# The mean square of a differential attention head: two transposes and a row sum, or two products with ones

## The chip, the cores and the metric

One core of one Trainium2 chip runs the whole program, one layer of a streaming encoder. The metric is the device time of one execution in microseconds, the median of three runs. In the text PE or TensorE is the matrix engine, DVE or VectorE the vector engine, ACT or ScalarE the activation engine, POOL or GpSimd the general engine, and SP the engine that issues most DMAs.

## The reference

The layer has parallel token mixers, a cross-attention and a gated MLP, over 512 tokens of width 1024 in float32. The change lies in the first mixer, the differential attention with four heads: two softmax maps of a head are subtracted, the difference multiplies the values, and the result of each head and token, 128 numbers, is normalised by its root mean square, with a gain per channel.

```python
def _rms_norm(x, g):
    xf = x.astype(jnp.float32)
    y = xf * lax.rsqrt(jnp.mean(xf * xf, axis=-1, keepdims=True) + EPS)
    return (y * g.astype(jnp.float32)).astype(x.dtype)
...
        p = jax.nn.softmax(jnp.where(mask, s, -jnp.inf), axis=-1)
        a = p[:, :, 0] - lam * p[:, :, 1]
        return jnp.einsum('bhqk,bkhe->bqhe', a.astype(v.dtype), v)
...
        ya = (_rms_norm(ya, diff_norm[l]) * (1.0 - lambda_init)).reshape(B, S, BR_W)
...
        br = jnp.stack([ya, yf, yc, ys], axis=2)
        proj = jnp.einsum('bsnc,ncd->bsnd', br, w_branch[l])
```

The normalised heads are branch a of four; each branch is projected, gated and summed.

## The kernel before

Every float32 matrix product is made of three TensorE products of rounded parts: a high part (rounded to the format that TensorE reads) and a low part (what the rounding left), high by high, high by low, low by high. `split` makes the parts: ScalarE copies to the high one, VectorE subtracts it to get the low one. Weights come in by DMA, are split and used, job after job; `run_blocks` fetches three jobs ahead.

Attention isn't a job of its own. The four heads of branch a are background tasks (`a_task`), put in a queue when their q and k columns are ready; between jobs `bg.tick()` lets at most two tasks take steps, by a clock of the TensorE work issued. The order of instructions on each engine is settled when the program is built, by a scheduler over the whole program; on the chip each engine takes its own list in that order and waits where an operand isn't ready.

A task has six steps. In steps 0 to 3 it makes scores of 128 queries against 128 to 512 keys (two maps, banks `sc`), reads them with mask and maximum (L831), takes exponentials (L836), scales (L840) and subtracts (L841). In steps 1 to 4 the difference is transposed (bank `tr`, L236) and split into `pth` and `ptl`. In steps 3 and 5 these multiply the values into one bank `av`, so that `av` at the end holds the head's output turned: 128 channels on the partitions, 512 tokens along the free dimension. The mean square is over the channels, and so over the partitions.

The kernel before turns it: the copy at L846 takes `av` to SBUF, four transposes bring the tokens to the partitions, ScalarE squares (L852), VectorE sums along the free dimension (L854), GpSimd adds EPS and raises to the power -0.5 (`rstd_of`, L268 and L271, 128 x 4), VectorE multiplies (L856), four transposes turn it back, and a split with the gain `half["dn"]` (L158 and L159) writes the branch's parts `y["a"]`, tiles `y8b`.

Buffers matter here. `e4()` gives one of three SBUF buffers of 128 x 2 x 512, which scores, differences and outputs of all heads share. There are two banks each of `mm`, `av`, `tr` and `sc`. While the heads run, gate and branch products use `mm` alone; when the heads are through, the products for the values of the second attention (`vf_jobs`) use `mm` and `av`, and then its tasks (`f_task`) begin, whose bias tiles GpSimd makes from rows `crows`, which it stores and loads by DMA (L943, L960, L990, L992). Branch a's projections (`gate_blocks(0, "a")`) come after the first q and k columns of that attention. GpSimd also clears parts of the `qk` tiles (L760).

Of the kernel before, what the change touches and what calls it, by code (L numbers as in the profile page):

```python
# [17 lines left out]
F32 = mybir.dt.float32  # L18
F32R = mybir.dt.float32r
AF = mybir.ActivationFunctionType  # L20
ALU = mybir.AluOpType
AX = mybir.AxisListType
# [3 lines left out]
P = 128  # L26
S = 512
D = 1024
NT = S // P
# [54 lines left out]
def hybrid_layer(ctx: ExitStack, tc: tile.TileContext, a: dict, out: bass.AP):  # L84
    nc = tc.nc
    V, A, G, PE, SP = nc.vector, nc.scalar, nc.gpsimd, nc.tensor, nc.sync
# [10 lines left out]
    def bank(tag=None):  # L97
        if tag is None:
            turn_of.n += 1
            tag = "av" if turn_of.shared and turn_of.n % 2 else "mm"  # L100
        return psum.tile([P, 512], F32, tag=tag, name=f"ps_{tag}", bufs=2)
# [13 lines left out]
    nhalf = gp.tile([P, 8], F32, name="nhalf")  # L115
    G.memset(nhalf[:, :4], -0.5)
    G.memset(nhalf[:, 4:], EPS)
    eps = nhalf[:, 4:]
# [33 lines left out]
    def split(ps, hi, lo, scale=None):  # L152

        if scale is None:
            A.copy(hi, ps)  # L155
            V.tensor_tensor(lo, ps, hi.bitcast(F32), ALU.subtract)  # L156
        else:
            A.activation(hi, ps, AF.Copy if isinstance(scale, float) else AF.Identity, scale=scale)  # L158
            V.scalar_tensor_tensor(lo, ps, scale, hi.bitcast(F32), ALU.mult, ALU.subtract)  # L159
# [71 lines left out]
    def matmul(ps, lhs, rhs, start, stop):  # L231
        PE.matmul(ps, lhs, rhs, start=start, stop=stop)  # L232
        bg.clock += max(int(math.prod(rhs.shape[1:])), 256) * 0.00042

    def transpose(ps, x, n=P):
        PE.transpose(ps, x, ident[:n, :n])  # L236
        bg.clock += 0.107
# [26 lines left out]
    def rstd_of(pool, parts, n=1):  # L264

        m = pool.tile([P, n], F32, tag="st_m", name="st_m", bufs=4)
        r = pool.tile([P, n], F32, tag="st_r", name="st_r", bufs=4)
        G.tensor_tensor(m, parts[0], eps[:, :n], ALU.add)  # L268
        for part in parts[1:]:
            G.tensor_tensor(m, m, part, ALU.add)  # L270
        G.tensor_tensor(r, m, nhalf[:, :n], ALU.pow)  # L271
        return r
# [33 lines left out]
    m1p = m1.__enter__()  # L306
# [6 lines left out]
    def e4(dtype=F32):  # L313
        return m1p.tile([P, 2, S], dtype, tag="e", name="e", bufs=3)
# [191 lines left out]
    half = {}  # L506
# [77 lines left out]
    def y8b():  # L584
        return m2bp.tile([P, 4, S], F32R, tag="y8b", name="y8b", bufs=2)

    acc = [m2p.tile([P, S], F32, tag=f"acc{m}", name=f"acc{m}") for m in range(NK)]
    y = {}
# [191 lines left out]
    def scores(ps, qk, c, q0, w):  # L780

        q = slice(q0, q0 + P)
        matmul(ps[:, :w], qk[:, c, q], qk[:, 2 + c, :w], True, False)
        matmul(ps[:, :w], qk[:, c, q], qk[:, 4 + c, :w], False, True)

    def to_keys_major(e, n, pt_h, pt_l, local):

        ps = bank("tr")
        for kt in range(n):
            transpose(ps[:, kt * P:(kt + 1) * P], e[:, kt * P:(kt + 1) * P])  # L790
        sl = slice(local * P, (local + 1) * P)
        split(ps[:, :n * P].rearrange("p (k c) -> p k c", k=n), pt_h[:, :n, sl], pt_l[:, :n, sl])

    def values(ps, terms, pt, half):


        n = 2 * half + 2
        for kt in range(n):
            q0 = P if kt == n - 1 else 0
            passes = terms(kt)  # L800
            for i, (v, p) in enumerate(passes):
                matmul(ps[:, half * 256 + q0:half * 256 + 256], v, pt[p][:, kt, q0:256],
                       kt == 0 and i == 0, kt == n - 1 and i == len(passes) - 1)

    def pt_tiles():
        return (m1p.tile([P, 4, 256], F32R, tag="pth", name="pth", bufs=2),
                m1p.tile([P, 4, 256], F32R, tag="ptl", name="ptl", bufs=2))


    def a_task(h, qk, v):  # L810
        es, pt, av = {}, None, None
        for step in range(6):
            if step in (3, 5):
                if av is None:
                    av = bank("av")
                vh, vl = (x[:, :, h * P:(h + 1) * P] for x in v[0])
                values(av, lambda kt: ((vh[:, kt], 0), (vh[:, kt], 1), (vl[:, kt], 0)), pt, step // 2 - 1)
            cost = 0.0
            if 1 <= step <= 4:
                if step in (1, 3):  # L820
                    pt = pt_tiles()
                to_keys_major(es.pop(step - 1)[:, 0], step, pt[0], pt[1], (step - 1) % 2)
                cost += 0.1 + 0.15 * step
            if step < 4:
                qt, w = step, (step + 1) * P
                e = es[qt] = e4()
                st = m1p.tile([P, 8], F32, tag="st8", name="st8", bufs=4)
                for c in range(2):
                    ps = bank("sc")
                    scores(ps, qk, c, qt * P, w)  # L830
                    V.tensor_tensor_reduce(e[:, c, :w], ps[:, :w], mask_a[:, S - w:], scale=1.0,  # L831
                                           scalar=-3.0e38, op0=ALU.add, op1=ALU.max,
                                           accum_out=st[:, c:c + 1])
                V.tensor_scalar(st[:, 2:4], st[:, 0:2], -HD ** -0.5, None, ALU.mult)
                for c in range(2):
                    A.activation(e[:, c, :w], e[:, c, :w], AF.Exp, bias=st[:, 2 + c:3 + c],  # L836
                                 scale=HD ** -0.5, accum_out=st[:, 4 + c:5 + c])
                V.reciprocal(st[:, 6:8], st[:, 4:6])
                V.tensor_scalar(st[:, 7:8], st[:, 7:8], lam, None, ALU.mult)
                A.activation(e[:, 1, :w], e[:, 1, :w], AF.Copy, scale=st[:, 7:8])  # L840
                V.scalar_tensor_tensor(e[:, 0, :w], e[:, 0, :w], st[:, 6:7], e[:, 1, :w], ALU.mult,  # L841
                                       ALU.subtract)
                cost += 0.6 + 0.0035 * w
            if step == 5:
                e = e4()
                A.copy(e[:, 0], av)  # L846
            yield cost, 3.5

        ps = bank("tr")
        for t in range(NT):  # L850
            transpose(ps[:, t * P:(t + 1) * P], e[:, 0, t * P:(t + 1) * P])
        A.activation(e[:, 1], ps, AF.Square, scale=1.0 / math.sqrt(P))  # L852
        ms = m1p.tile([P, NT], F32, tag="ms4", name="ms4", bufs=2)
        V.tensor_reduce(ms, e[:, 1].rearrange("p (t c) -> p t c", t=NT), AX.X, ALU.add)  # L854
        r = rstd_of(m1p, [ms], NT)
        V.tensor_tensor(e[:, 0].rearrange("p (t c) -> p t c", t=NT),  # L856
                        ps.rearrange("p (t c) -> p t c", t=NT),
                        r.unsqueeze(2).to_broadcast([P, NT, P]), ALU.mult)
        yield 1.5, 3.5
        ps2 = bank("tr")  # L860
        for t in range(NT):
            transpose(ps2[:, t * P:(t + 1) * P], e[:, 0, t * P:(t + 1) * P])
        if "a" not in y:
            y["a"] = (y8b(), y8b())
        split(ps2, y["a"][0][:, h], y["a"][1][:, h], half["dn"])
        yield 0.6, 0.0


    crows = dram.tile([8, S], F32, name="crows")
# [192 lines left out]
    def mixer_jobs():  # L1062
# [23 lines left out]
        for h, n in enumerate((0, 2, 4, 6)):  # L1086
            yield from qk_jobs(O_AQ, O_AK, h, lambda qk, h=h: bg.add(a_task(h, qk, va), "a"))
            if n:
                yield then(lambda: bg.drain("conv"))
            for _ in range(n):  # L1090
                yield next(gc)
# [651 lines left out]
```

## Time and profile before

| | |
|---|---|
| Time, median of three runs | 1065.24 us (1065.16 to 1066.46) |
| Profiled execution: span | 1064.1 us, 1.1 us less than that median |
| TensorE busy | 1052.2 us, 99% of the span |
| VectorE, ScalarE, GpSimd busy | 796.6, 497.5, 147.8 us |
| HBM traffic | 142 GB/s over the span |

The profile is of one execution. Busy time is that of an engine's own instructions; in the slices a digit is the busy share in tenths of one fortieth of the span, 26.6 us. In a timeline row the bracket gives the idle time of the engine ahead of the row and what ended it. A group's row gives the busy time of all its instructions, the mean of one in ns, and the idle time ahead of them. The profile lists no time of this execution other than its span; what lies around the span is taken from the median.

### The profile page before, as it was taken

The numbers are of one execution on the slowest core, as the hardware profiler recorded it, in microseconds if no ns is written. First come the engines' busy times: TensorE is split into PE (matmuls) and PEld (weight loads), VectorE is DVE, ScalarE is ACT, GpSimd is POOL, SyncE is SP. The second block draws the span as 40 slices with busy tenths as digits, with TensorE's granted clock in tenths as the row PEclk, the third lists the DMA queues.
The fourth block names the chain that finished last, engine by engine and source line by source line (L and its number), as shares of the span: only waits on it lengthen the run. The fifth ranks groups of instructions, "written<-read, shape, count | busy, mean of one in ns | idle before, by whom it ended". The sixth has DMA issues, their size and how long they took to land.

```text
span 1064.1 us, 14583 instructions
## 1 busy us (share of the span) xinstructions
PE 1052.2 (99%) x5375; PEld 895.3 (84%) x5375; DVE 796.6 (75%) x1262; ACT 497.5 (47%) x819; POOL 147.8 (14%) x249
## 2 busy tenths in 40 slices
PE   9999999999999999999999999999999999999997
PEld 8888888888888978888888899999888888888886
DVE  6999997567666357776675888786778787777796
ACT  5322222367465255645443565664333333445662
POOL 4000000000001015332110031021111211111001
PEclk9999999999999999999999999999999999999999
DMA  8954333322222242332344754225576766725672
GB/s 264 300 155 103 104 96 99 97 82 80 80 80 63 58 139 79 100 99 80 119 125 140 268 159 120 80 75 190 180 228 218 237 219 216 235 82 179 204 219 81
DMA packets 162108, 152.58 MB, mean 143 GB/s; under 512 B 5567, under 2 KB 135212, under 8 KB 162037
## 3 DMA queue, kind: packets, MB, share of 16 engines
q1 hardware_dynamic: 152995, 119.91, 37.4%
q10 hardware_dynamic: 6482, 23.21, 5.8%
q0 software_dynamic: 2560, 8.54, 2.8%
q8 instruction: 42, 0.69, 0.3%
q14 instruction: 29, 0.24, 0.1%
HBM read 133.79 MB, written 17.84 MB: 142 GB/s over the span
## 4 chain that ended last, share of the span: by engine, by line
PE 93%; issue 3%; DMA 1%; ACT 1%; DVE 1%; POOL 0%; POOLq 0%; DVEq 0%; SPq 0%; ACTq 0%
PE ps_mm L232 50%; PE ps_av L232 29%; PE ps_sc L232 7%; PE ps_tr L232 4%; PE ps_tr L236 3%; DMA wide<-in_w_out 1%; DMA ck<-crows 0%; PE ps_mm L384 0%; DMA crows<-e 0%; PE ps_sc L389 0%; DVE nt L281 0%; POOL st_r L271 0%; ACT hth L432 0%; ACT wa L412 0%; ACT wh L190 0%
## 5 line engine op out<-in xcount | busy, mean ns | idle before, releaser
L190 ACT CAST wh<-wr 128x1024 fp32r<-128x1024 f32 (+1 forms) x142 | 148.7, 1050 | 273.1 <-PE ps_mm L232 181.1
L191 DVE TENSOR_TENSOR wl<-wr,wh 128x1024 fp32r<-128x1024 f32 (+1 forms) x142 | 178.2, 1256 | 89.4 <-ACT wh L190 89.1
L232 PE MATMUL ps_mm<-hth,wh 128*128 128x512 f32 (+1 forms) x616 | 231.4, 382 | 0.6 <-DVE qk L765 0.3
L232 PE MATMUL ps_mm<-htl,wh 128*128 128x512 f32 (+1 forms) x616 | 230.2, 380 | 0.0
L232 PE MATMUL ps_mm<-hth,wl 128*128 128x512 f32 (+1 forms) x616 | 229.9, 380 | 0.0
L232 PEld LDWEIGHTS ps_mm<-hth,wh 128*128 128x128 f32 x616 | 114.1, 188 | 21.7 <-ACT hth L155 0.8
L232 PEld LDWEIGHTS ps_mm<-hth,wl 128*128 128x128 f32 x616 | 114.0, 188 | 21.1
L232 PEld LDWEIGHTS ps_mm<-htl,wh 128*128 128x128 f32 x616 | 114.2, 188 | 20.4
L232 PE MATMUL ps_av<-hth,wh 128*128 128x512 f32 (+1 forms) x328 | 122.6, 374 | 0.0
L232 PE MATMUL ps_av<-htl,wh 128*128 128x512 f32 (+1 forms) x328 | 122.5, 374 | 0.0
L232 PE MATMUL ps_av<-hth,wl 128*128 128x512 f32 (+1 forms) x328 | 122.5, 373 | 0.0
L664 DVE SCALAR_TENSOR_TENSOR y<-y,par,y 128x482 f32<-128x482 f32 (+29 forms) x120 | 83.9, 743 | 0.2
L232 PEld LDWEIGHTS ps_av<-hth,wl 128*128 128x128 f32 x328 | 61.6, 188 | 10.9
L232 PEld LDWEIGHTS ps_av<-htl,wh 128*128 128x128 f32 x328 | 61.6, 188 | 10.9
L232 PEld LDWEIGHTS ps_av<-hth,wh 128*128 128x128 f32 x328 | 61.7, 188 | 10.7
L1536 DVE TENSOR_TENSOR wl<-dw,wh 128x1024 fp32r<-128x1024 f32 x32 | 40.2, 1261 | 12.2 <-ACT wh L1535 12.0
L1535 ACT CAST wh<-dw 128x1024 fp32r<-128x1024 f32 x32 | 33.4, 1051 | 22.6 <-PE ps_tr L232 7.5
L990 POOL TENSOR_SCALAR fbias<-ck,cq 128x128 f32<-128x128 f32 (+3 forms) x32 | 27.5, 865 | 69.0 <-DVE st L996 61.8
L1484 ACT ACTIVATE th<-c 128x512 f32<-128x512 f32 x22 | 13.9, 631 | 48.5 <-DVE c L594 45.6
L155 ACT CAST pth<-ps_tr 128x512 fp32r<-128x512 f32 (+3 forms) x56 | 23.4, 448 | 22.0 <-PE ps_tr L236 21.8
L594 DVE SCALAR_TENSOR_TENSOR c<-ps_mm,par,c 128x510 f32<-128x510 f32 (+1 forms) x44 | 32.7, 744 | 0.7
L156 DVE TENSOR_TENSOR ptl<-ps_tr,pth 128x512 fp32r<-128x512 f32 (+3 forms) x56 | 27.9, 512 | 6.0 <-ACT pth L155 5.7
(471 smaller groups left out, 2105.2 us busy)
## 6 DMA issues: line engine op xcount, KB each, us to landing
wr<-in_w_up SPq DMA_DIRECT2D x44, 512.0 KB
wr<-in_w_in SPq DMA_DIRECT2D x38, 512.0 KB
wr<-in_w_gate SPq DMA_DIRECT2D x32, 512.0 KB
wp<-in_w_down ACTq DMA_DIRECT2D x22, 512.0 KB
sums<-wp ACTq DMA_DIRECT2D x22, 512.0 KB
dw<-sums SPq DMA_DIRECT2D x44, 256.0 KB
wr<-in_w_branch SPq DMA_DIRECT2D x16, 512.0 KB
wide<-in_w_out SPq DMA_DIRECT2D x12, 512.0 KB
```

Source lines behind the costliest of these rows:

```text
L155: A.copy(hi, ps)
L156: V.tensor_tensor(lo, ps, hi.bitcast(F32), ALU.subtract)
L190: order(A.copy(hi, raw[:, :n]))
L191: low.tensor_tensor(lo, raw[:, :n], hi.bitcast(F32), ALU.subtract)
L232: PE.matmul(ps, lhs, rhs, start=start, stop=stop)
L236: PE.transpose(ps, x, ident[:n, :n])
L594: ins = V.scalar_tensor_tensor(dst[:, s:], src[:, :S - s], w(k), dst[:, s:], ALU.mult, ALU.add)
L664: ins = V.scalar_tensor_tensor(dst[:, s:], src[:, :S - s], pc("conv_dw", k * 4 + j), dst[:, s:], ALU.mult, ALU.add)
L990: G.tensor_scalar(bias[:, :w], ck[j][:, :w], -1.0, cq[:, qt, head:head + 1], ALU.mult, ALU.add)
L1484: A.activation(th, c[:, 0], AF.Tanh, scale=0.5)
L1535: A.copy(hi, x)
L1536: V.tensor_tensor(lo, x, hi.bitcast(F32), ALU.subtract)
```

## The change

In step 5 the head's output isn't copied. ScalarE squares `av` with the factor 1/128 into `e`, rounds it to the high part in a second buffer `sq`, and VectorE makes the low part. Two products with a 128 x 128 tile of ones (written by GpSimd into the place in `y["a"]` that the head's result will take later) sum both parts over the partitions, in a bank `sc`; every partition then holds the mean square of all 512 tokens. ScalarE adds EPS on the way to SBUF, GpSimd raises the 128 x 512 tile to -0.5, and VectorE multiplies `av` by the gain and this tile, and the result is split. The eight transposes, the row sum and `rstd_of` are gone; `av` is read a second time at the end.

```diff
             if step == 5:
-                e = e4()
-                A.copy(e[:, 0], av)
+                e, sq = e4(), e4(F32R)
+                if "a" not in y:
+                    y["a"] = (y8b(), y8b())
+                G.memset(y["a"][0][:, h, :P].bitcast(F32), 1.0)
+                A.activation(e[:, 0], av, AF.Square, scale=1.0 / math.sqrt(P))
+                A.copy(sq[:, 0], e[:, 0])
+                V.tensor_tensor(sq[:, 1], e[:, 0], sq[:, 0].bitcast(F32), ALU.subtract)
             yield cost, 3.5
 
-        ps = bank("tr")
-        for t in range(NT):
-            transpose(ps[:, t * P:(t + 1) * P], e[:, 0, t * P:(t + 1) * P])
-        A.activation(e[:, 1], ps, AF.Square, scale=1.0 / math.sqrt(P))
-        ms = m1p.tile([P, NT], F32, tag="ms4", name="ms4", bufs=2)
-        V.tensor_reduce(ms, e[:, 1].rearrange("p (t c) -> p t c", t=NT), AX.X, ALU.add)
-        r = rstd_of(m1p, [ms], NT)
-        V.tensor_tensor(e[:, 0].rearrange("p (t c) -> p t c", t=NT),
-                        ps.rearrange("p (t c) -> p t c", t=NT),
-                        r.unsqueeze(2).to_broadcast([P, NT, P]), ALU.mult)
-        yield 1.5, 3.5
-        ps2 = bank("tr")
-        for t in range(NT):
-            transpose(ps2[:, t * P:(t + 1) * P], e[:, 0, t * P:(t + 1) * P])
-        if "a" not in y:
-            y["a"] = (y8b(), y8b())
-        split(ps2, y["a"][0][:, h], y["a"][1][:, h], half["dn"])
-        yield 0.6, 0.0
+        ps = bank("sc")
+        for i in range(2):
+            matmul(ps, y["a"][0][:, h, :P], sq[:, i], i == 0, i == 1)
+        A.activation(e[:, 0], ps, AF.Identity, bias=eps[:, :1])
+        G.tensor_tensor(e[:, 0], e[:, 0], nhalf[:, :1].to_broadcast([P, S]), ALU.pow)
+        yield 0.8, 3.5
+        V.scalar_tensor_tensor(e[:, 1], av, half["dn"], e[:, 0], ALU.mult, ALU.mult)
+        split(e[:, 1], y["a"][0][:, h], y["a"][1][:, h])
+        yield 2.0, 0.0
```

## The prediction

> **What bounds the kernel now.** I read the page first: busy times, the slices, then the chain that ended last.
>
> ```profile
> span 1064.1 us, 14583 instructions
> PE 1052.2 (99%) x5375; PEld 895.3 (84%) x5375; DVE 796.6 (75%) x1262; ACT 497.5 (47%) x819; POOL 147.8 (14%) x249
> POOL 4000000000001015332110031021111211111001
> PEclk9999999999999999999999999999999999999999
> PE 93%; issue 3%; DMA 1%; ACT 1%; DVE 1%; POOL 0%; POOLq 0%; DVEq 0%; SPq 0%; ACTq 0%
> ```
>
> TensorE is busy for 99% of the span and carries 93% of the chain; GpSimd is nearly idle. Whatever keeps TensorE fed costs nothing, and whatever takes its next instruction away costs its full length. 0.2% (about 2 us) is what a measurement of this kernel can tell from no change.
>
> Next the timeline of GpSimd around the four differential heads, where the change works. Columns: start, length, engine, line, instruction, and in brackets the idle time before it.
>
> ```profile
> 265.45 1.09 POOL L760 MEMSET qk<- 64x512 f32 x2 [14.87 <-issue]
> 274.02 1.46 POOL L271 TENSOR_TENSOR st_r<-st_m,nhalf 128x4 f32<-128x4 f32 x1
> 292.98 1.01 POOL L271 TENSOR_TENSOR st_r<-st_m,nhalf 128x4 f32<-128x4 f32 x1
> 329.77 1.01 POOL L271 TENSOR_TENSOR st_r<-st_m,nhalf 128x4 f32<-128x4 f32 x1
> 356.81 1.01 POOL L271 TENSOR_TENSOR st_r<-st_m,nhalf 128x4 f32<-128x4 f32 x1
> 388.39 0.57 POOL L943 DMA_DIRECT2D crows<-e  x1 [30.58 <-DVE e L942]
> ```
>
> The four powers to -0.5 (one a head, four columns each) lie 274 to 358 us, with GpSimd idle between them. The change makes each 512 columns wide. So the whole forecast hangs on what a power costs per column.
>
> **The price of the power.** The groups by form (busy us, mean ns) and two single rows:
>
> ```profile
> L271 POOL TENSOR_TENSOR st_r<-st_m,nhalf 128x1 f32<-128x1 f32 x30 | 19.7, 659 | 1.6
> L271 POOL TENSOR_TENSOR st_r<-st_m,nhalf 128x4 f32<-128x4 f32 x4 | 4.5, 1122 | 0.3
> L268 POOL TENSOR_TENSOR st_m<-ms,nhalf 128x4 f32<-128x4 f32 x4 | 0.8, 202 | 66.9 <-DVE ms L854 49.6 <-DVE st L834 17.2
> L415 POOL TENSOR_TENSOR wa<-e,wa 128x512 fp32r<-128x512 f32 x4 | 5.1, 1297 | 1.4 <-ACT wa L412 1.4
> 16.65 0.55 POOL L271 TENSOR_TENSOR st_r<-st_m,nhalf 128x1 f32<-128x1 f32 x1
> 17.16 0.19 POOL L268 TENSOR_TENSOR st_m<-st_s,nhalf 128x1 f32<-128x1 f32 x1
> ```
>
> An addition costs 0.19 us for one column and 0.20 for four: width is free there. The power costs 0.55 us for one and 1.01 for four (three of four; the fourth, 1.46, lifts the mean): 0.153 us for each further column, and the means give the same slope, (1122 - 659) / 3 = 154 ns. Carried to 512 columns: 0.55 + 511 x 0.153 = 78.7 us. No row shows a wide power, so I bound it: below by a two-operand 512-column subtraction, 1.30 us; above by all of 1.01 us scaled by 128, 129 us. I take 78.7, the row nearest in operation; the subtraction is another operation, whose own slope is not that of the power.
>
> The Trainium skill, page "GPSIMD Engine Reference", section "3.1 Elementwise — side-by-side cycle accounting", counts about 2.6 cycles an element at 1.2 GHz for a two-operand elementwise operation; by it, as an estimate, the power would take about 1.1 us and the kernel would come out as in rival A. The subtraction's row fits that rule; the power's rows don't.
>
> **Part 1, TensorE's own work.** Out go eight transposes a head, in come two 512-column products. The chain of before in order of time (start, length, count) has their pitch:
>
> ```profile
> 254.93 3.40 PE ps_mm L232 x15
> 258.33 0.71 PE ps_sc L232 x4
> 270.04 0.77 PE ps_tr L236 x7
> 320.51 1.23 PE ps_av L232 x11
> ```
>
> A 512-column product is 0.227 us, a 384-column one 0.18, a transpose 0.11, a product of 128 to 264 columns 0.11. So 0.88 - 0.45 = 0.43 us less a head, 1.7 us in all. This is the only gain.
>
> **Part 2, the small steps.** Gone from ScalarE and VectorE are the copy, square, reduction, multiplication and the scaled split; new are the square, the two-part rounding of it, the addition of EPS, one multiplication and a split. The nearest rows:
>
> ```profile
> L846 ACT COPY e<-ps_av x4: 575/587/589, 266.8 to 351.6; 128x512 f32<-128x512 f32 x4
> L158 ACT ACTIVATE y8b<-ps_tr,s_dn x4: 672/688/690, 281.6 to 361.6; 128x512 fp32r<-128x512 f32 x4
> L155 ACT CAST y8b<-e x4: 612/620/621, 82.0 to 130.2; 128x512 fp32r<-128x512 f32 x4
> L156 DVE TENSOR_TENSOR y8b<-e,y8b x4: 705/713/722, 84.9 to 132.3; 128x512 fp32r<-128x512 f32 x4
> L841 DVE SCALAR_TENSOR_TENSOR e<-e,st 128x512 f32<-128x512 f32 x4 | 3.0, 749 | 0.3 <-ACT e L840 0.3
> ```
>
> ScalarE goes from three passes of 0.6 to 0.7 us to four, VectorE keeps three of about 0.7: under 1 us a head, beside engines at 47% and 75%. Counted at nothing, since TensorE's products cover it. The memsets of ones (0.2 us each) stand far ahead on GpSimd, also at nothing.
>
> **Part 3, what waits for the power.** In the order in which the changed kernel is built, GpSimd runs the four powers as one chain, and three things hang on each: the head's `av` bank, which now stays in use until the last multiplication (before, the copy at L846 freed it); its `e` buffer, one of three; and VectorE's queue, where that multiplication waits with the next head's score reads behind it. Head 2's first score read stands behind head 0's multiplication, and its reading frees the `sc` bank for head 1's sum. So the power of head 1 can't begin before that of head 0 has ended, and so for heads 1 and 2. Between two powers lie multiplication 0.75, split 0.62 + 0.71, two score reads with their two exponentials (their groups stand under rival A, with means of 0.49 and 0.56 us over all widths; for 128 and 256 columns I take 1.7 and 2.2 in all), and the EPS addition 0.69: 4.5 and 5.0 us. Head 3's input is ready in time; only three memsets (1.6 us) lie before its power. Behind the last come 0.75 + 0.62 = 1.4 us until the first product of branch a. Length of the chain: 4 x 78.7 + 4.5 + 5.0 + 1.6 + 1.4 = 327 us.
>
> What TensorE can do meanwhile is read off that order, with the pitches above:
> - behind head 0's power, up to head 1's sum: 252 products of 512 columns and 68 narrow ones, 57.2 + 7.6 = 64.8 us
> - behind the powers of heads 1 and 2, up to the first `av` product of the f values, which needs head 2's bank: 14 wide, 8 of 384, 116 narrow, 3.2 + 1.4 + 13.0 = 17.6 us. The remaining attention of heads 2 and 3 stands here with few other products between
> - behind head 3's power, up to the first branch-a product: 144 wide, 108 narrow, 32.7 + 12.1 = 44.8 us
>
> 327 - 127 = 200 us are left in which TensorE has nothing to do. GpSimd's DMAs of `crows` and the f bias are queued behind the last power too, but come before TensorE needs more.
>
> **Part 4, TensorE's clock.** The same six products at the start and a few microseconds later:
>
> ```profile
> 1.33 2.93 PE L384 MATMUL ps_mm<-e,ones 128*128 128x256 f32 x6 [1.33 <-DVE e L335]
> 6.69 1.46 PE L384 MATMUL ps_mm<-e,ones 128*128 128x256 f32 x6
> ```
>
> From rest they take twice as long. Four long rests follow here, each with about 1.5 us of such a restart, up to 3 if a slow stretch is longer; some of it falls where ScalarE and VectorE are late anyway. I take 4 us, between 0 and 12. The Trainium skill, page "TensorE: Matmul & The Clock Gate", section "What's actually happening", has the array at half its clock after an idle window of about 3.4 us and for about 3.4 us of work; by that the four restarts would be at most 7 us. The rows agree in the factor, though the slices' granted clock, quoted above, shows full speed there.
>
> **Sum.** The profiled span of 1064.1 us lies 1.1 us under the median of 1065.24; I keep that distance. 1065.2 - 1.7 + 200 + 4 = 1267.5, so 1268 us.
>
> **Rivals.** For a power of p us the same count gives: behind head 0, p + 1 - 65 where positive; behind heads 1 and 2, 2p + 10 - 18, but at least about 22 (rival A); behind head 3, p + 3 - 45, but at least about 5.
>
> A, the power costs as an addition does. For it: an addition's width is free. Against: the two power rows. It would still be slower, because the attention of heads 2 and 3 now stands packed:
>
> ```profile
> L831 DVE CUSTOM_DVE_ANT_0 e<-ps_sc,mask_a 128x128 f32<-128x128 f32 (+3 forms) x32 | 14.7, 488 | 4.7 <-PE ps_sc L232 4.7
> L836 ACT ACTIVATE e<-e,st 128x128 f32<-128x128 f32 (+3 forms) x32 | 17.7, 556 | 6.8 <-DVE st L834 6.8
> L840 ACT ACTIVATE e<-e,st 128x128 f32<-128x128 f32 (+3 forms) x16 | 9.0, 562 | 5.3 <-DVE st L839 5.2
> L841 DVE SCALAR_TENSOR_TENSOR e<-e,st 128x128 f32<-128x128 f32 (+3 forms) x16 | 8.7, 548 | 2.2 <-ACT e L840 2.1
> ```
>
> These four groups alone are 50.1 us for four heads, 25 for two, one after the other in each step; with the small steps and the transposed splits it is about 40 us against 17.6 of products: some 22 lost, and 5 more behind head 3. 1065 - 2 + 27 = 1090 us, between 1075 and 1100.
>
> B, a wide power runs at half the price a column, about 40 us (its loop may fill better than four columns show). 0 + 72 + 5: 1065 - 2 + 77 = 1140 us. Nothing in the trace speaks for it but that no width above four is shown.
>
> C, the work above one addition grows by groups of four, (1.01 - 0.20) / 4 = 0.20 us a column, 104 us. 40 + 200 + 62: 1065 - 2 + 302 + 4 = 1369 us. Against: the first column would then be as dear as four, and it is not.
>
> D, the other side: the power is cheap and TensorE finds its queue full throughout, so that only part 1 counts: 1065.2 - 1.7 = 1063.5 us. It decides so only if a power stays under about 10 us and the packed attention runs with gate products between. The idle GpSimd speaks for it; the built order, with 17.6 us of products beside two heads of attention, against.
>
> **How the numbers follow.** Forecast 0.75, with its own range 1250 to 1290 (a power of 75 to 83 us, a restart of 0 to 12). A 0.06, B 0.10, C 0.06, D 0.03. For 8 in 10 I reach into B's upper half (a power of 53 us gives 0 + 98 + 11, about 1176 with the restart) and a little above the linear price (86 us, about 1300): 1175 to 1300. Faster is D alone; the chance of no difference is a remainder between D and A: 0.02, 0.01, 0.97.
>
> **What would show it.** In the profile after: four GpSimd rows of 128x512 near 79 us each, nearly end to end from about 277 us (the 274 of before and a longer chain ahead of it) to about 604, GpSimd's busy time up by about 312 us; four long waits of TensorE, near 15, twice 60 to 70 with short ones between, and near 30 us, each released by the steps behind a power; TensorE's products otherwise at 0.227 us; all as before after the first branch-a product. A power of a few microseconds, or TensorE waiting on something else in that stretch, would make it wrong.

## The result, and the profile after

The changed kernel takes 1275.87 us (median of four runs, 1274.94 to 1276.07) where the kernel before takes 1065.23 (1065.16 to 1066.46) beside it. The ratio is 1.198, 95% interval 1.196 to 1.200: slower by 210.6 us. The profiled executions have spans of 1273.2 and 1064.1 us, 209.1 us apart.

The page of the changed kernel: busy times, the slices of TensorE, of GpSimd and of the granted clock (one fortieth of the span is 31.8 us here), and the shares of the chain that ended last.

```profile
PE 1072.9 (84%) x5351; PEld 906.7 (71%) x5351; DVE 800.7 (63%) x1262; ACT 501.4 (39%) x823; POOL 469.1 (37%) x249
PE   9999999999740060295599999999999999999997
POOL 3000010039989989999733200030211211111001
PEclk9999999999955565598799999999999999999999
PE 71%; POOL 19%; issue 8%; DVE 1%; ACT 0%; POOLq 0%; DVEq 0%; ACTq 0%
```

In a stretch of some 340 us GpSimd's digits stand at 7 to 9. TensorE's fall there to 0 in three slices and to between 2 and 7 in six others, and stay at 9 in two. GpSimd, which had 0% of the chain, holds 19%. Outside that stretch the rows look like before's.

GpSimd's timeline in that stretch (start, length, engine, line, instruction; in brackets the idle time before it; left out are three short memsets, ahead of the third and of the fourth power):

```profile
277.19 81.95 POOL L858 TENSOR_TENSOR e<-e,nhalf 128x512 f32<-128x512 f32 x1 [11.09 <-issue]
363.71 81.92 POOL L858 TENSOR_TENSOR e<-e,nhalf 128x512 f32<-128x512 f32 x1 [4.58 <-ACT e L857]
...
450.73 81.92 POOL L858 TENSOR_TENSOR e<-e,nhalf 128x512 f32<-128x512 f32 x1 [3.94 <-issue]
...
534.23 81.91 POOL L858 TENSOR_TENSOR e<-e,nhalf 128x512 f32<-128x512 f32 x1
```

Four powers of 81.9 us, nearly end to end from 277.19 to 616.14 us, on an engine whose four powers took 4.5 us before. What TensorE does meanwhile is in the rows that follow its long waits (the number in brackets is the wait), and in the windows by stage (length, then the busy time of PE, PEld, DVE, ACT and POOL, granted clock, DMA share, GB/s):

```profile
361.68 1.22 PE L232 MATMUL ps_sc<-e,y8b 128*128 128x512 f32 x2 [20.55 <-DVE st L831]
448.41 1.19 PE L232 MATMUL ps_sc<-e,y8b 128*128 128x512 f32 x2 [67.30 <-DVE st L831]
533.48 0.59 PE L232 MATMUL ps_av<-wh,hth 128*128 128x264 f32 x1 [59.21 <-DVE e L860]
617.62 1.65 PE L232 MATMUL ps_mm<-y8b,wh 128*128 128x512 f32 x3 [27.31 <-ACT y8b L155]
```

```profile
277.00:361.00 84.00, 64.13 (x315) 54.11 (x313) 28.27 (x32) 21.35 (x28) 81.95 (x1) 0.90 0.25 75
361.00:446.00 85.00, 14.75 (x51) 10.79 (x51) 12.50 (x48) 11.44 (x33) 82.23 (x2) 0.52 0.00 0
446.00:533.00 87.00, 19.37 (x87) 15.86 (x87) 12.11 (x35) 11.23 (x27) 82.94 (x4) 0.56 0.00 0
533.00:618.00 85.00, 53.85 (x271) 46.06 (x272) 26.06 (x42) 24.68 (x35) 83.62 (x5) 0.82 0.22 62
```

The four waits make 174.4 us. None of them names GpSimd: TensorE waits for VectorE and ScalarE. The engine behind them is found one step further back, in what the last multiplication (L860) waited for:

```profile
  POOL e L858: 168.9, 4
```

In the two middle stages TensorE works 14.75 of 85 and 19.37 of 87 us, at a granted clock of 0.52 and 0.56; VectorE and ScalarE are idle too, and almost nothing moves on the DMA queues. Everything stands behind GpSimd.

### The profile page after: what moved, and what is told of

Read it like the earlier page. It is cut to its first block, busy times and chain, and to the rows that moved or that the text cites. A ratio compares the mean times of both kernels' runs of the same rounds, so it can differ in the third digit from the quotient of the medians.

```text
span 1273.2 us, 14547 instructions
## 1 busy us (share of the span) xinstructions
PE 1072.9 (84%) x5351; PEld 906.7 (71%) x5351; DVE 800.7 (63%) x1262; ACT 501.4 (39%) x823; POOL 469.1 (37%) x249
## 4 chain that ended last, share of the span: by engine, by line
PE 71%; POOL 19%; issue 8%; DVE 1%; ACT 0%; POOLq 0%; DVEq 0%; ACTq 0%
PE ps_mm L232 35%; PE ps_av L232 23%; POOL e L858 19%; PE ps_sc L232 6%; PE ps_tr L232 3%; PE ps_tr L236 2%; PE ps_mm L442 0%; PE ps_av L442 0%; PE ps_mm L384 0%; PE ps_sc L389 0%; DVE wl L191 0%; DVE e L860 0%; ACT y8b L155 0%; DVE o L1629 0%; ACT wh L190 0%
## 5 line engine op out<-in xcount | busy, mean ns | idle before, releaser
L858 POOL TENSOR_TENSOR e<-e,nhalf 128x512 f32<-128x512 f32 x4 | 327.7, 81924 | 19.6 <-issue 15.0
L860 DVE SCALAR_TENSOR_TENSOR e<-ps_av,s_dn,e 128x512 f32<-128x512 f32 x4 | 3.0, 751 | 168.9 <-POOL e L858 168.9
L232 PE MATMUL ps_av<-wh,hth 128*128 128x512 f32 (+2 forms) x74 | 26.0, 363 | 62.5 <-DVE e L860 59.2
L232 PE MATMUL ps_sc<-e,y8b 128*128 128x512 f32 x8 | 4.0, 572 | 87.9 <-DVE st L831 87.9
L155 ACT CAST y8b<-e 128x512 fp32r<-128x512 f32 x8 | 4.9, 618 | 177.6 <-DVE e L860 175.7
L232 PEld LDWEIGHTS ps_av<-wh,hth 128*128 128x128 f32 x74 | 15.0, 203 | 64.7 <-DVE e L860 59.4
```

The costliest lines, as they stand in the source:

```text
L858: G.tensor_tensor(e[:, 0], e[:, 0], nhalf[:, :1].to_broadcast([P, S]), ALU.pow)
L860: V.scalar_tensor_tensor(e[:, 1], av, half["dn"], e[:, 0], ALU.mult, ALU.mult)
```

## The experiments

All start from the changed kernel, except the last. Each kernel's order of instructions is built anew, so the work that lies beside a power differs from one to the next.

**The root on ScalarE.** The rest of the change stays.

```diff
-        A.activation(e[:, 0], ps, AF.Identity, bias=eps[:, :1])
-        G.tensor_tensor(e[:, 0], e[:, 0], nhalf[:, :1].to_broadcast([P, S]), ALU.pow)
+        A.activation(e[:, 0], ps, AF.Ln, bias=eps[:, :1])
+        A.activation(e[:, 0], e[:, 0], AF.Exp, scale=-0.5)
```

> The root is taken on ScalarE (logarithm of the mean square plus EPS, then the exponential of -0.5 times it, two passes over 128 x 512) and GpSimd does none of it; the rest is as in the changed kernel. Theory (the power on GpSimd, 81.92 us each, is the whole loss): two passes of about 0.7 us in place of 81.92, TensorE never rests long, so 1065.2 less the 1.7 us of the transposes, with small losses: 1062 to 1068 us, and the four long TensorE waits are gone. Rival A (what costs is that the heads stand packed and that each hands on to the next): about 1090 us, with the waits behind the score reads still there. Rival of the functions (changing between logarithm and exponential costs ScalarE time): gaps or long rows at those two passes; at over 5 us a head it would show as 1075 us or more.

Measured: 1062.96 us against 1065.82 for the kernel before on the same chip, ratio 0.9974 (0.9966 to 0.9983): faster than both kernels, by 2.9 us against before (1.8 to 3.6 by the interval). What differs is the medians: single runs of the kernel before went there from 1061.51 to 1067.12 us, and of this one from 1061.89 to 1063.86. The whole loss hangs on the one instruction. The span is 1062.1 us; the busy times of its page, and then the two groups of table loads on ScalarE (busy us, mean ns of one):

```profile
PE 1051.0 (99%) x5351; PEld 893.6 (84%) x5351; DVE 798.5 (75%) x1262; ACT 513.0 (48%) x835; POOL 143.6 (14%) x245
```

```profile
L857 ACT ACT_TABLE_LOAD x4 | 5.1, 1283 | 1.0 <-PE ps_sc L232 1.0
L858 ACT ACT_TABLE_LOAD x4 | 5.1, 1283 | 0.1
```

TensorE is back at 99%. The rival of the functions holds in part: each change between logarithm and exponential loads a table, 1283 ns, eight times. That is 10.3 us of ScalarE and costs nothing, because ScalarE, busy 48% of the span, isn't what TensorE waits for.

The Trainium skill, page "ScalarE: Activation LUTs", section "Table sets: the hidden batching unit", has logarithm and exponential in one set, so that one load would do for both; in this run each change had its load.

**A multiplication in place of the power.**

```diff
-        G.tensor_tensor(e[:, 0], e[:, 0], nhalf[:, :1].to_broadcast([P, S]), ALU.pow)
+        G.tensor_tensor(e[:, 0], e[:, 0], nhalf[:, :1].to_broadcast([P, S]), ALU.mult)
```

> The 128 x 512 operation on GpSimd is a multiplication by the same operand instead of a power, so the root is left out; place, width, engine and operands are the same. Theory (the price of the power per column): the four operations take 1.3 us each, as the 512-column subtraction on that engine did, instead of 81.92, and the time is 1063 to 1068 us. Rival (any 512-column operation of GpSimd in this place is slow, or the handing over between heads costs): over 1090 us.

Measured: 1063.92 us, ratio 0.9991 (0.9977 to 1.0004). The group of the multiplications (busy us, mean ns of one, then idle time before):

```profile
L858 POOL TENSOR_TENSOR e<-e,nhalf 128x512 f32<-128x512 f32 x4 | 4.2, 1041 | 62.2 <-ACT e L857 51.1 <-issue 11.1
```

1.04 us where the power takes 81.92, on the same engine, with the same operands, in the same place of the program; the kernel leaves the root out. So neither GpSimd as such nor the row of steps around it is dear, but this operation. The estimate of 1.1 us that the prediction worked out from the Trainium skill, page "GPSIMD Engine Reference", section "3.1 Elementwise — side-by-side cycle accounting", is near the 1.04 us of the multiplication and short by a factor of 74 for the power.

**Half the columns.**

```diff
-        G.tensor_tensor(e[:, 0], e[:, 0], nhalf[:, :1].to_broadcast([P, S]), ALU.pow)
+        G.tensor_tensor(e[:, 0, :256], e[:, 0, :256], nhalf[:, :1].to_broadcast([P, 256]), ALU.pow)
```

> The power is taken over 256 of the 512 columns; the other tokens keep the mean square without a root. Theory (0.160 us a column, one chain): four rows of 41 us; by the prediction's count 0 behind head 0, 2 x 41 + 10 - 18 = 74 behind heads 1 and 2, 5 behind head 3, so 1065 - 2 + 79 = 1142 us, from 1127 if the packed stretch loses less. Rival (loss in proportion to the power): half of 210 us, 1170 us. Rival (a fixed price for an instruction, width free): 1276 us.

Measured: 1126.49 us, ratio 1.0572 (1.0553 to 1.0591), at the lower end of what was expected (1142, from 1127) and far from both rivals. Halving the powers takes away 149 of 211 us, not half: cover comes off first. The group of the powers, and the windows of this kernel (columns as above):

```profile
L858 POOL TENSOR_TENSOR e<-e,nhalf 128x256 f32<-128x256 f32 x4 | 164.5, 41124 | 26.8 <-issue 15.0 <-ACT e L857 11.8
```

```profile
270.00:318.00 48.00, 48.00 (x223) 39.95 (x222) 23.14 (x33) 19.09 (x28) 40.95 (x1) 1.00 0.29 84
...
330.00:371.00 41.00, 21.15 (x122) 18.31 (x120) 14.49 (x42) 12.45 (x30) 41.00 (x1) 0.74 0.10 26
...
376.00:417.00 41.00, 16.98 (x83) 14.18 (x83) 8.95 (x25) 8.95 (x22) 40.80 (x1) 0.62 0.00 1
417.00:460.00 43.00, 38.31 (x208) 33.21 (x209) 19.75 (x35) 16.86 (x25) 42.89 (x6) 0.95 0.30 86
```

The price is linear: 41.12 and 81.92 us, 0.159 us for each column between them. Head 0's power is hidden whole, as the count had it (TensorE busy 48 of 48 us), and head 3's costs 4.7 us where the count said 5. In the middle the count, 74 us, was too high: TensorE stands idle 19.9 and 24.0 us beside the two powers and some 3 between them, 47 in all. What it does there runs at 0.74 and 0.62 of the clock, and that makes its busy time 13 us longer over the span (1063.5 against 1050.3 us with the multiplication). 47 + 5 + 13 = 65 us, near the 62.6 by which the span exceeds that with the multiplication (1061.7). The 17.6 us of cover were counted for the order with 512 columns; in this one more work lies beside the second power (122 instructions, where the changed kernel has 51).

**The bank freed early.**

```diff
                 V.tensor_tensor(sq[:, 1], e[:, 0], sq[:, 0].bitcast(F32), ALU.subtract)
+                A.copy(e[:, 1], av)
...
-        V.scalar_tensor_tensor(e[:, 1], av, half["dn"], e[:, 0], ALU.mult, ALU.mult)
+        V.scalar_tensor_tensor(e[:, 1], e[:, 1], half["dn"], e[:, 0], ALU.mult, ALU.mult)
```

> ScalarE copies av to SBUF behind the square, and the last multiplication reads the copy, so that the av bank is free before the power. Theory (the chain of the four powers ends last, and what is freed inside it only lets TensorE run ahead to the next wait): the time stays at 1276 us within 5, the 59 us wait of the av product goes, and another wait, at the first product of branch a, grows by about as much. Rival (the held av bank costs by itself): 59 us less, about 1217 us.

Measured: 1276.3 us, ratio to before 1.1975 (1.1954 to 1.1997): no change. TensorE's waits (in all, times, longest), and the windows of the last two powers:

```profile
PE ps_mm L232 <- ACT y8b L155: 93.4, 2, 79.2
PE ps_sc L232 <- DVE st L831: 87.9, 2, 67.3
```

```profile
446.00:533.00 87.00, 66.01 (x347) 56.40 (x347) 32.99 (x71) 34.82 (x61) 82.95 (x4) 0.87 0.21 61
533.00:618.00 85.00, 3.91 (x11) 2.26 (x11) 4.68 (x6) 1.24 (x2) 83.89 (x5) 0.50 0.00 0
```

The 59 us wait of the `av` product is gone, TensorE works 66 us beside the third power instead of 19, and then has 4 us left beside the fourth instead of 54. The sum of the waits is 181 us where it was 174. The wait that was taken away named a bank; its length was set by GpSimd, and it came back at the next door.

**One power alone**, for head 0 (shown) and, in a second kernel, for head 3; the other heads take the root on ScalarE.

```diff
-        A.activation(e[:, 0], ps, AF.Identity, bias=eps[:, :1])
-        G.tensor_tensor(e[:, 0], e[:, 0], nhalf[:, :1].to_broadcast([P, S]), ALU.pow)
+        A.activation(e[:, 0], ps, AF.Identity if h == 0 else AF.Ln, bias=eps[:, :1])
+        if h == 0:
+            G.tensor_tensor(e[:, 0], e[:, 0], nhalf[:, :1].to_broadcast([P, S]), ALU.pow)
+        else:
+            A.activation(e[:, 0], e[:, 0], AF.Exp, scale=-0.5)
```

> The power on GpSimd for head 0 alone (81.92 us); heads 1 to 3 take the root on ScalarE by logarithm and exponential. Theory (a power costs its length less the TensorE work that the order leaves beside it): by the prediction's count 82 + 1 - 65 = 18 us behind head 0 alone, so 1063 + 18 = 1081 us, and up to 1107 where the three heads behind it then stand packed. Rival (each power costs the same, a quarter of the 210 us): 1063 + 53 = 1116 us. Rival (one power is hidden, only the chain of four costs): 1063 us.

> The power on GpSimd for head 3 alone; heads 0 to 2 take the root on ScalarE. Theory (length less cover): 82 + 3 - 45 = 40 us behind head 3, all of it in one wait of TensorE at the first product of branch a: 1063 + 40 = 1103 us, and none behind the other heads. Rival (each power costs the same): 1116 us. Rival (only the chain of four costs): 1063 us.

Measured: head 0 alone 1108.5 us, ratio 1.0418 (1.0397 to 1.044); head 3 alone 1104.95 us, ratio 1.038 (1.036 to 1.04). The second meets its forecast of 1103; the first lies just above the upper end of its range, 1107. Head 3's kernel: the power takes 81.95 us from 362.80 us on; the window of the work beside it, and TensorE's longest wait:

```profile
363.00:413.00 50.00, 48.70 (x257) 41.22 (x255) 23.14 (x38) 23.82 (x34) 50.00 (x1) 1.00 0.34 98
```

```profile
PE ps_mm L232 <- ACT y8b L155: 33.1, 1, 33.1
```

Some 50 us of work lie beside the power, where 45 were counted in the order of the changed kernel, then TensorE waits 33.1 us for the end. The span, 1103.1 us, is 41.0 above that with no power (1062.1), and the count said 40. Of the 8 us that are not in this wait, 4.9 are TensorE's busy time (1055.9 against 1051.0 us), longer at the lower clock behind it; the other 3 no single wait names. Head 0's kernel:

```profile
277.00:360.00 83.00, 64.31 (x316) 54.27 (x314) 27.77 (x31) 20.92 (x27) 81.95 (x1) 0.92 0.26 76
360.00:420.00 60.00, 46.17 (x239) 38.66 (x240) 29.46 (x97) 37.11 (x78) 2.59 (x5) 0.69 0.03 8
```

```profile
PE ps_sc L232 <- DVE st L831: 24.8, 5, 20.6
```

A wait of 20.6 us where the count said 18, and then a second loss. In the 60 us after the power TensorE is idle for 13.8 us, 12 of them behind that wait, and works at a clock of 0.69, which makes its busy time 14 us longer over the span (1065.1 against 1051.0 us). The span is 44.8 us above that with no power, so 24 lie beyond the wait: 14 of busy time and 10 more of idle time over the whole span. That fits the mechanism of the prediction's rival A, the attention of the heads packed behind one another with too few products between, which it priced at 22 us for two heads; here three heads stand behind the power. No run separates it from other reasons. The two kernels lose nearly the same, 44.8 and 41.0 us, but not in the same way: a wait of 20.6 us and 24 behind it, or a wait of 33.1 and 8. So the two times alone would not refute an equal price for each power; that the cost isn't in proportion is shown by the kernels with 256 and with 64 columns. The two kernels together lose 86 of the 211 us; if the losses add, 125 are left to the two powers in the middle, which have little work beside them. A power has no price of its own for the kernel: it costs its length less the cover at its place, and what it crowds together behind it.

**Sixty-four columns.**

```diff
-        G.tensor_tensor(e[:, 0], e[:, 0], nhalf[:, :1].to_broadcast([P, S]), ALU.pow)
+        G.tensor_tensor(e[:, 0, :64], e[:, 0, :64], nhalf[:, :1].to_broadcast([P, 64]), ALU.pow)
```

> The power over 64 of the 512 columns (the other tokens keep the mean square without a root). Theory (0.160 us a column, cover of 18 to 65 us a power): four rows of 10.2 us, all nearly covered: 1064 to 1070 us. This is also the point from which the rival D of the prediction was to hold (a power under about 10 us). Rival (packed heads cost by themselves): 1090 us.

Measured: 1067.73 us, ratio 1.0025 (1.0012 to 1.0039).

```profile
L858 POOL TENSOR_TENSOR e<-e,nhalf 128x64 f32<-128x64 f32 x4 | 42.1, 10528 | 54.6 <-ACT e L857 43.5 <-issue 11.1
```

At 10.5 us a power the kernel is 2.6 us slower than before, and some 5 slower than with the root on ScalarE. With 1.04 us an operation (the multiplication) the interval still holds no difference. So a power begins to cost before its length reaches the 18 to 65 us of products that were counted beside it. No wait of TensorE in this kernel is longer than 1.4 us, but the stretch with the heads shows where it falls back:

```profile
250.00:420.00 170.00, 165.13 (x880) 141.02 (x879) 100.71 (x228) 90.98 (x177) 57.35 (x33) 0.99 0.27 80
```

TensorE does 880 instructions here, where it does 914 in the same 170 us of the kernel with the multiplication (busy 167.37 us, granted clock 1.00). Over the whole span 2.6 of the 4.9 us between the two (1066.6 and 1061.7 us) are idle time in short waits, and 2.3 are longer busy time. Which step each short wait hangs on stays open.

**The power by itself**, in the kernel before, early in the program where nothing soon waits for GpSimd.

```diff
+        base, res = (m1p.tile([P, S], F32, tag="fbias", name=f"curve{i}", bufs=2) for i in range(2))
+        G.memset(base, 2.0)
+        for n in (2, 8, 32, 128, 256):
+            G.tensor_tensor(res[:, :n], base[:, :n], nhalf[:, :1].to_broadcast([P, n]), ALU.pow)
+        G.tensor_tensor(res[:64, :128], base[:64, :128], nhalf[:64, :1].to_broadcast([64, 128]), ALU.pow)
+        G.tensor_tensor(res[:, :128], base[:, :128], eps[:, :1].to_broadcast([P, 128]), ALU.pow)
+        G.tensor_tensor(res[:, :256], base[:, :256], nhalf[:, :1].to_broadcast([P, 256]), ALU.mult)
```

> The kernel before, with eight more GpSimd operations early in the program, on constants: powers to -0.5 of 128 partitions by 2, 8, 32, 128 and 256 columns, one of 64 partitions by 128 columns, one of 128 x 128 to another exponent (EPS), and a multiplication of 128 x 256. Theory (a first cost and a price per column): with 81.92 at 512, 41.12 at 256 and 1.01 at 4 columns, 0.7, 1.6, 5.4, 20.7 and 41.1 us; the 64 partitions by 128 columns also 20.7, since partitions run side by side. Rival (a price per element over all partitions): 10 us for 64 partitions. Rival (the price hangs on the exponent or the values): the power to EPS differs from 20.7. The multiplication: under 1.3 us.

Measured, the groups of these operations (L644 the widths, L645 the 64 partitions, L646 the other exponent, L647 the multiplication):

```profile
L644 POOL TENSOR_TENSOR curve<-curve,nhalf 128x2 f32<-128x2 f32 x1 | 0.7, 717 | 10.0 <-PE ps_tr L236 10.0
L644 POOL TENSOR_TENSOR curve<-curve,nhalf 128x8 f32<-128x8 f32 x1 | 1.7, 1668 | 0.1
L644 POOL TENSOR_TENSOR curve<-curve,nhalf 128x32 f32<-128x32 f32 x1 | 5.9, 5913 | 0.1
L644 POOL TENSOR_TENSOR curve<-curve,nhalf 128x128 f32<-128x128 f32 x1 | 21.0, 21037 | 0.1
L644 POOL TENSOR_TENSOR curve<-curve,nhalf 128x256 f32<-128x256 f32 x1 | 41.5, 41462 | 0.1
L645 POOL TENSOR_TENSOR curve<-curve,nhalf 64x128 f32<-64x128 f32 x1 | 21.9, 21854 | 0.1
L646 POOL TENSOR_TENSOR curve<-curve,nhalf 128x128 f32<-128x128 f32 x1 | 23.2, 23222 | 0.0
L647 POOL TENSOR_TENSOR curve<-curve,nhalf 128x256 f32<-128x256 f32 x1 | 0.9, 934 | 0.1
```

The price grows with the columns from the first on: from 2 to 8 columns (1668 - 717) / 6 = 159 ns each, from 128 to 256 (41462 - 21037) / 128 = 160 ns. Half the partitions cost the same, 21.9 against 21.0 us, so it is a price per column and not per element. The other exponent took 23.2 us; whether the values matter by that tenth, one row can't say. The single time of this kernel is 1066.92 us, within the runs of the kernel before beside it (1062.62 to 1067.24), with 117 us more of GpSimd's work in it: a GpSimd that nobody waits for costs nothing that this run can show.

## Why the prediction was right

**What bounds.** It said that only what takes TensorE's next instruction away costs, and that the whole forecast hangs on the price of a power. Both are shown: with the root on ScalarE the loss is gone, and with 117 us of GpSimd's work out of the way of others the time hardly moves.

**The price.** 81.92 us, forecast 78.7, within the bounds of 1.30 and 129 us. This is the term that was mis-sized most: 3.2 us a power, 12.9 in all. The slope came from two short rows, 0.55 and 1.01 us, and was 0.153; it is 0.159. That a slope from one and four columns holds to 512 was an assumption, which no row of the kernel before could bear out; the widths from 2 to 512 now do. That the means of the two groups gave 154 ns as well was partly luck, since both hold rows lifted to 1.4 or 1.5 us, one of the four and three of the thirty. The step itself, to carry the slope of the same operation to 512 columns rather than take the duration of a nearer width from another operation, is what made the forecast.

**The chain.** Forecast 327 us from the first power to the first product of branch a; it is 617.62 - 277.19 = 340.4. The price gives 12.9 of the 13.4 us of difference. The gaps, forecast 4.5, 5.0, 1.6 and 1.4, are 4.57, 5.10, 1.58 and 1.48 us. Four powers are 328 of the 340 us. Of the three things that the prediction hung on each power, the run with the freed bank shows that the `av` bank doesn't set the length; the `e` buffer and VectorE's queue were not tested apart.

**The cover.** 127 us. The counts are borne out: the windows have 315 instructions of TensorE beside the first power, 51 + 87 beside the next two and 271 beside the fourth, where 320, 138 and 252 were counted. The waits, forecast near 15, twice 60 to 70 and near 30 us, are 20.6, 67.3, 59.2 and 27.3. What the work is worth in time was put too low. At 277.19 us, where the first power starts, TensorE has done 1355 instructions in the changed kernel and 1356 in the kernel before, so both are about equally far. From there to the first product of branch a, the changed kernel's window and then before's (whose first branch-a product starts at 413.33 us):

```profile
277.19:617.62 340.43, 151.53 (x722) 126.30 (x720) 78.56 (x154) 68.51 (x123) 330.74 (x10) 0.70 0.12 34
277.19:413.33 136.14, 133.46 (x744) 115.49 (x744) 78.38 (x181) 68.21 (x133) 18.46 (x35) 1.00 0.31 88
```

```profile
413.33 0.62 PE L232 MATMUL ps_mm<-y8b,wh 128*128 128x512 f32 x2
```

By the count, before's stretch would be the cover and the 1.7 us of part 1, 128.7 us long; it is 136.1. So the stretch grew by 204.3 us, where the chain as measured less 128.7 would be 211.7: the cover was 7.4 us too small. Of these, 2.7 are idle time that TensorE has in before's stretch, and the rest is its products there, which take longer than the count by pitches has them. "All as before" behind the first branch-a product holds within 5 us: the rest takes 1273.2 - 617.62 = 655.6 us, and took 1064.1 - 413.33 = 650.8.

**Part 1 and the small steps.** TensorE's busy time in the kernel with the root on ScalarE is 1051.0 against 1052.2 us: 1.2 us less where 1.7 were forecast. The small steps cost nothing that shows: that kernel is 2.9 us faster than before, with even the table loads hidden. The measured gain is larger than the 1.2 us: the spans differ by 2.0, and the other 0.8 is less idle time of TensorE. Which of its short waits make that up is not shown.

**The clock.** TensorE's busy time in the changed kernel rose by 20.7 us, to 1072.9, though it has less to do. The windows say why: a granted clock of 0.52 and 0.56 in the two sparse stages. By the two windows above, 18.1 us of the 20.7 lie between the first power and the first product of branch a (151.53 against 133.46 us, for 22 instructions less), in a stretch whose length GpSimd's chain sets, and cost nothing. Where TensorE goes back to full work it costs something, and its timeline shows how much:

```profile
619.07 0.63 PE L232 MATMUL ps_mm<-y8b,wl 128*128 128x512 f32 x1
619.50 0.63 PE L232 MATMUL ps_mm<-y8b,wh 128*128 128x512 f32 x1
619.92 0.63 PE L232 MATMUL ps_mm<-y8b,wl 128*128 128x512 f32 x1
620.48 0.56 PE L232 MATMUL ps_mm<-hth,wh 128*128 128x512 f32 x1
620.87 0.39 PE L232 MATMUL ps_mm<-htl,wh 128*128 128x512 f32 x1
621.11 0.39 PE L232 MATMUL ps_mm<-hth,wl 128*128 128x512 f32 x1
```

```profile
617.62 8.65 PE ps_mm L232 x30
```

Up to 620.9 us, 3.3 us after the wait, products start 0.39 to 0.56 us apart, and then 0.23 to 0.24. The last line is from the chain in order of time: 30 products in 8.65 us instead of 30 x 0.227 = 6.81, so this restart cost 1.8 us; the 1.5 of the prediction is near. The other three restarts run into further waits. The term of 4 us was too high by about 2. The Trainium skill, page "TensorE: Matmul & The Clock Gate", section "What's actually happening", has half the clock for about 3.4 us of work after an idle window; the 3.3 us agree. The estimate of at most 7 us for four restarts that was worked out from it would have been too high by more.

**The sum.** 200 + 4 - 1.7 = 202.3 us were forecast. With 12.9 more for the price, 0.5 for the gaps and 2.2 less for the restart it would be 213.5; the spans differ by 209.1. The windows place the difference: 7.4 us of cover more than counted, and behind the first branch-a product 4.8 us lost where the restart explains 1.8, so 3.0 that no run places. That the forecast came within 8 us is in part luck, since the price and the cover, both too low, miss in opposite directions.

**The rivals.** A (the power as cheap as an addition) fell on its price: 1.04 us is what a multiplication takes. Its mechanism, the packed heads, fits what head 0's kernel loses, but a cheap operation doesn't bring it about: in the order built around the multiplication there are products between (TensorE is busy for 167.37 of the 170 us with the heads), and the time is 1063.9, not 1090. B (half price) and C (groups of four columns) fell on the measured slope. D (a cheap power, only part 1 counts) was right for a power that is cheap: 1063.5 forecast, 1063.9 with the multiplication (a difference to before that the interval can't tell from none) and 1063.0 with the root on ScalarE. Its limit of about 10 us may be too high: at 10.5 us, in the kernel with 64 columns, 2.6 us are lost already. Where the loss begins stays open, since no operation between 1.04 and 10.5 us was run.

## What to carry to other kernels

An operation's price at one width says nothing of its slope: find two widths of the same operation in the trace, carry the slope to the new width, and do that before anything else when a change widens a tile on an engine that looks idle. Then ask what work lies beside it at its place; a wait on a buffer that ends with such an operation isn't the buffer's. Here the idea of the change was sound and one choice inside it was not: with the root taken by logarithm and exponential on ScalarE it beats both kernels, by 2.9 us and by 213.

## What the runs showed of the hardware

- A power on GpSimd costs about 0.16 us a column from 2 to 512 columns (between neighbouring widths of the run by itself, 2 to 256 columns, 0.158 to 0.177, and 0.158 on to the 512 of the changed kernel); 64 partitions cost no less than 128 (21.85 against 21.04 us for 128 columns); a multiplication of 128 x 512 there costs 1.04 us in all.
- Alternating logarithm and exponential on ScalarE loaded a table at each change, 1.283 us; where nothing else held it, the next activation began 1.29 us after the load did.
- In the two stretches where TensorE worked 17 and 22% of the time its granted clock was 0.52 and 0.56. After its wait of 27.3 us products started 0.39 to 0.56 us apart for 3.3 us, and 0.23 to 0.24 after that.
